# Laying the RWKV-7 units out by pairs of heads, with an issue order that counts changes of tile shape

## The chip, the core and the metric

The kernel runs on one core of a Trainium2 chip. Five engines work side by side: TensorE (PE, with its weight loads as PEld), VectorE (DVE), ScalarE (ACT), GpSimd (POOL) and the DMA queues that SyncE (SP) issues. Each engine takes its instructions in the order in which they were issued, and semaphores hold an instruction back until its inputs are there. The metric is the device time of one execution in microseconds; lower is better.

## The reference, cut to what matters

The kernel computes a two-layer trunk for 256 tokens of width 1024: an RWKV-7 time mixing with a dense SwiGLU, then a dilated attention with a mixture of experts. The change is in the time mixing, which has 16 heads of 64 columns:

```python
    def step(state, inp):
        r_t, w_t, k_t, v_t, a_t, b_t = inp
        sa = jnp.einsum('bhvk,bhk->bhv', state, a_t)
        state = state * w_t[:, :, None, :] + sa[..., None] * b_t[:, :, None, :] + v_t[..., None] * k_t[:, :, None, :]
        return state, jnp.einsum('bhvk,bhk->bhv', state, r_t)

    s0 = jnp.zeros((B, H, N, N), jnp.float32)
    _, y = lax.scan(step, s0, seq_in)
```

The kernel does not step through the 256 tokens. It takes them in chunks of 64: inside a chunk the recurrence becomes a triangular 64x64 matrix for each head that is inverted (E below), and between chunks a 64x64 state for each head is handed on (ST below).

## The kernel before, in words

All engine work goes through a small recorder, the class `Engine`, whose `call` emits the instruction; so nearly every row of the profile carries its line, L190, and rows are told apart by tile names. The recorder also keeps a planner's clock for each engine: `cost` estimates an instruction, `start` says when its inputs would be ready. The work around the change is written as tasks (Python generators) that yield the engine and the tiles that their next step needs. `spin` takes, again and again, the task whose next step could start first by that clock, and a task's order number decides ties. So the planner's estimates alone fix the order of the instructions on each engine.

In this stage `spin` runs eight units (`unit`, from L869), four at a time in four lanes; a new unit starts when a lane is free. A unit is one group of four heads (256 columns, `c_` = 0 to 3) and one half of the tokens (128 tokens, `t` = 0 or 1). A lane has one PSUM bank (`lps`). Around the units run the projections of r and v (`rv_task`, tiles x0h, x0l, x2h, x2l into mmb), four of the adaLN rows (`ada_lane` with `ada_pe`, tiles rawa and cs_act), the splitting of fp32 weights into a high and a low part (whi on ACT, wlo on DVE), the output projection (`wo_task`, tiles ygh and ygl) and what the next stage needs (`pre_task`, `pn_task`). `wo_task` begins only when the ada rows are done and `gate` is there.

A unit goes through these steps, all in 128 partitions, where the upper and the lower 64 partitions are the two chunks of 64 tokens:

- A, R, and the products BKn of b and k are made elementwise; `transpose` turns A and R into ART, and BKn into BKT. BKn is written on DVE as four pieces of 64x256.
- The scores: BKT times ART, eight products of 64 rows by 128 columns (K = 64, tile names ART,BKT). The four of one half of the rows go into the lane's bank and are masked into SM on DVE; then the four of the other half follow in the same bank.
- The inverse: E starts from SM, and four rounds of two product groups follow (T,SM into X, then E,X into E), each of eight 64x64 products, and a last round in 32x32 tiles. Chunk 0 works in array quadrant (0,0) and chunk 1 in quadrant (64,64), in turn.
- The state, chunk after chunk: SM times SV (plus ART times the state ST) gives U; E times U goes into SV; BKn times SV, added to ST and scaled by pcm, is the next ST; SM times SV plus ART times ST gives Y. The four heads of a chunk all write to the same 64 output partitions, those of the chunk.
- Y is normalized on DVE, multiplied with the gate (lga with g2t, and the last 32 rows as a product of 32 rows, tile names w2t,lw), transposed, and split into ygh and ygl.

An fp32 product of the code stands as two rows MATMUL in the trace, a transpose and a product of split weights (fp32r) as one.

Elsewhere the same recorder orders the attention stage.

## Time and profile before

| | us |
|---|---|
| three runs | 1843.07, 1843.85, 1847.41 (median 1843.85) |
| profiled execution, its own time | 1846.92 |
| its span | 1845.2 |
| PE busy | 1715.7 (93%) |
| DVE busy | 1497.0 (81%) |
| ACT busy | 1120.4 (61%) |
| POOL busy | 296.6 (16%) |

The span runs from the first to the last instruction; 1.7 us of the execution lie around it. By the tile names of the trace, the time mixing runs from about 40 us to 370 us, the dense SwiGLU to about 590, the attention to about 825, and the experts to 1835. Matmuls overlap in their pipeline and each has a row of at least 0.2 us, so a busy PE can still take more work; what a product costs in a row of equal ones is read from the distance of the starts.

### The profile page before, as it was taken

How to read it: one execution, taken by the hardware profiler on the slowest of the kernel's cores; microseconds unless marked ns; L12 is line 12 of the kernel's file. 1: busy time of each engine (PE TensorE's matmuls, PEld its weight loads, DVE VectorE, ACT ScalarE, POOL GpSimd, SP SyncE). 2: the span in 40 equal slices, each digit the busy share in tenths (PEclk: the TensorE clock that was granted, in tenths of full speed). 3: DMA queues.
4: the chain of work that ended last, by engine and by line, in shares of the span. 5: the costliest groups of instructions: out<-in, count | busy, mean ns of one | idle time of the engine just before them, and what ended most of it. 6: DMA issues, size and time to landing. Idle time of an engine off the chain costs nothing. (4 is left out here: it accounts for less than half of the span.)

```text
span 1845.2 us, 26366 instructions
## 1 busy us (share of the span) xinstructions
PE 1715.7 (93%) x9828; PEld 1368.3 (74%) x9828; DVE 1497.0 (81%) x2044; ACT 1120.4 (61%) x1447; POOL 296.6 (16%) x222
## 2 busy tenths in 40 slices
PE   6998998869998888979999999999999999999896
PEld 3676776558876666778888888888788787788674
DVE  2786786389886768579899898998888988988888
ACT  3443342236553656438777777877777777777674
POOL 0012222044532785250000000000000000000200
PEclk8998998889998999979999999999999999999998
DMA  9551153559894574568999999999999999999880
GB/s 330 155 160 30 54 164 116 150 189 357 296 354 151 194 256 154 195 230 293 334 352 368 357 349 380 348 360 332 345 368 340 352 345 349 352 344 359 311 320 24
DMA packets 213564, 498.94 MB, mean 270 GB/s; under 512 B 14634, under 2 KB 28818, under 8 KB 213428
## 3 DMA queue, kind: packets, MB, share of 16 engines
q1 hardware_dynamic: 212564, 494.03, 75.7%
q0 software_dynamic: 864, 3.15, 0.5%
q8 instruction: 79, 1.29, 0.3%
q14 instruction: 57, 0.47, 0.1%
HBM read 496.07 MB, written 1.06 MB: 269 GB/s over the span
## 5 line engine op out<-in xcount | busy, mean ns | idle before, releaser
L190 DVE TENSOR_TENSOR wlo<-raw,whi 128x1024 fp32r<-128x1024 f32 x800 | 991.6, 1277 | 138.0 <-ACT whi L190 123.7
L190 ACT CAST whi<-raw 128x1024 fp32r<-128x1024 f32 x808 | 823.9, 1048 | 291.9 <-PE mmb L190 221.2
L190 PE MATMUL mmb<-wlo,xeh 128*128 128x512 f32 x896 | 355.9, 397 | 5.9 <-DVE wlo L190 5.2
L190 PE MATMUL mmb<-whi,xeh 128*128 128x512 f32 x896 | 352.5, 394 | 0.0
L190 PE MATMUL mmb<-whi,xel 128*128 128x512 f32 x896 | 351.6, 392 | 0.0
L190 PEld LDWEIGHTS mmb<-wlo,xeh 128*128 128x128 f32 x896 | 168.4, 188 | 48.3 <-DVE wlo L190 14.9
L190 PEld LDWEIGHTS mmb<-whi,xeh 128*128 128x128 f32 x896 | 168.4, 188 | 34.2 <-ACT whi L190 0.2
L190 PEld LDWEIGHTS mmb<-whi,xel 128*128 128x128 f32 x896 | 168.4, 188 | 32.6
L190 PE MATMUL psb<-wlo,ah 128*128 128x512 f32 x448 | 176.7, 394 | 1.5 <-DVE wlo L190 1.5
L190 PE MATMUL psb<-whi,al 128*128 128x512 f32 x448 | 174.7, 390 | 0.0
L190 PE MATMUL psb<-whi,ah 128*128 128x512 f32 x448 | 161.8, 391 | 0.0
L190 POOL TENSOR_TENSOR macc<-macc,gate 128x1024 f32<-128x1024 f32 x2 | 5.7, 2889 | 924.8 <-ACT gate L190 924.8
L190 POOL TENSOR_TENSOR acc<-acc,raw 128x512 f32<-128x512 f32 (+1 forms) x62 | 128.2, 2082 | 74.2 <-DVE acc L190 42.9
L190 PEld LDWEIGHTS psb<-wlo,ah 128*128 128x128 f32 x448 | 84.1, 188 | 24.6 <-DVE wlo L190 6.2
L190 PEld LDWEIGHTS psb<-whi,ah 128*128 128x128 f32 x448 | 83.5, 188 | 18.8 <-ACT whi L190 1.6
L190 PEld LDWEIGHTS psb<-whi,al 128*128 128x128 f32 x448 | 84.2, 188 | 16.4
L190 PE MATMUL mmb<-whi,f_xl 128*128 128x512 f32 (+1 forms) x192 | 72.1, 375 | 1.1 <-DVE f_xl L190 1.1
L190 PE MATMUL mmb<-whi,f_xh 128*128 128x512 f32 (+1 forms) x192 | 72.7, 379 | 0.0
L190 PE MATMUL mmb<-wlo,f_xh 128*128 128x512 f32 (+1 forms) x192 | 72.0, 375 | 0.2 <-DVE wlo L190 0.2
L190 ACT CAST ah<-psb 128x512 fp32r<-128x512 f32 x56 | 32.6, 583 | 60.3 <-PE psb L190 60.2
L190 ACT ACTIVATE e_s<-mmb 128x512 f32<-128x512 f32 x56 | 33.5, 599 | 44.8 <-PE mmb L190 44.8
L190 DVE TENSOR_TENSOR e_s<-e_s,mmb 128x512 f32<-128x512 f32 x56 | 38.2, 683 | 22.5 <-PE mmb L190 22.2
(417 smaller groups left out, 2589.3 us busy)
## 6 DMA issues: line engine op xcount, KB each, us to landing
raw<-in_moe_w_gu_dram SPq DMA_DIRECT2D x192, 1024.0 KB, 6.6
raw<-in_moe_w_down_dram SPq DMA_DIRECT2D x83, 1024.0 KB, 6.1
raw<-in_moe_w_gu_dram SPq DMA_DIRECT2D x60, 512.0 KB, 7.0
raw<-in_moe_w_down_dram SPq DMA_DIRECT2D x56, 512.0 KB, 6.0
raw<-in_ada_w_dram SPq DMA_DIRECT2D x37, 512.0 KB, 5.3
rawa<-in_ada_w_dram SPq DMA_DIRECT2D x35, 512.0 KB, 4.2
raw<-in_ada_w_dram SPq DMA_DIRECT2D x15, 1024.0 KB, 7.8
raw<-in_ffn_w_gu_dram SPq DMA_DIRECT2D x21, 512.0 KB, 5.3
```

What stands on the lines that cost most here:

```text
L190: return fn(*a, **kw)
```

## The change

Each lane's unit keeps its tiles and its steps. What is different:

- The two halves of the partitions hold two pairs of heads in place of the two chunks. In the inverse and the state, heads 0 and 1 of a unit work in one half of the array and heads 2 and 3 in the other, so that products that follow each other alternate between the two halves. The state's BKn times SV is four products of 64 output partitions in place of two of 128, and the sums with ST and the decay are done in halves of 64x128 by DVE; pcm is gone, and GpSimd clears SV and ST.
- The products b and k are made in 128x256 (Bf, Kf) and transposed together with A and R. The scores of the two row halves go into two PSUM banks in turn (the lane's own and mmb 2, which one unit at a time may hold, `bank2`).
- BKn is now copied from Bf and Kf in eight pieces of 64x128, SV from v in four, Y from the bank in four, and the E times U result by DVE and ACT, half each.
- The gate's last 32 rows stand in a zeroed 128-row tile (xh), so that their product has the full shape.
- The ada rows are issued in pairs, 16 rows of MATMUL in one go, with order number 3.5 (103 before); the r and v projections also have 3.5.
- `wo_task` also waits until all units have their scores, and `pre_task` takes its turn for the bank mmb 2.
- The planner adds 170 ns to a product whose tile shape differs from the last one (`CHG`), adds 170 ns to the ready time of a PE step whose hinted shape differs from the current one (`SHP`), makes DVE slower while GpSimd is at work (`GPF`), and no longer discounts alternating tiles in its count of PE activity.

```diff
+    CHG, GPF, SHP = 170, 0.6, 170
...
+                shp = tuple(32 if v <= 32 else 64 if v <= 64 else 128 for v in (k, m))
+                if shp != ham.get("shape"):
+                    ham["shape"] = shp
+                    start0, start = start, start + CHG
+                    grp["all"] = max([grp["all"]] + list(grp.values())) + CHG
+                    return self.pe(op, o, passes, n, k, m, col, cold, n0, start) + CHG
...
+            for q in range(0, 8, 2):
+                rws = [ada_raw(i, q + j) for j in range(2)]
+                yield PE, "128x32", rws[0], rws[1]
...
+        yield V, ta, kkr
+        Bf, Kf = kkr, Q
+        V.scalar_tensor_tensor(Bf, ta, 1.0, kkr, op0=OP.add, op1=OP.mult)
+        yield V, k2, Q
+        V.tensor_tensor(Kf, k2, Q, op=OP.mult)
+        yield lambda: not bank2[0]
+        bank2[0] = 1
+        yield PE, "128x128", A, R, Bf, Kf
...
+        pss = [lps((128, 2, 2, 128)), mmt(2, (128, 2, 2, 128))]
+        for ch in range(2):
+            for pr in range(2):
+                for par in range(2):
+                    sl = slice(par * 64, par * 64 + 64)
+                    PE.matmul(pss[par][:, ch, pr], BKT[sl, pr, ch].rearrange("q a t -> q (a t)"),
+                              ART[sl, pr, ch].rearrange("q a t -> q (a t)"), start=True, stop=True)
...
+        def each():
+            for ch in range(2):
+                for hh in range(2):
+                    for hp in range(2):
+                        yield slice(hp * 64, hp * 64 + 64), ch, 2 * hp + hh, ch * 2 + hh
...
+                for src, d in ((Bf, hp), (Kf, 1 - hp)):
+                    e = pick([SC, V], src)
+                    yield e, src
+                    (SC.copy if e is SC else V.tensor_copy)(BKn[d * 64:d * 64 + 64, ch, cs_], src[s_, cs_])
...
+        def products(ps, ch, a, st):
+            for hh in range(2):
+                for hp in range(2):
+                    h = 2 * hp + hh
+                    PE.matmul(ps[hp * 64:hp * 64 + 64, hh], SM[:, ch, h, a * 64:a * 64 + 64],
+                              SV[:, ch, h * 64:(h + 1) * 64], start=hh == 0, stop=st is None and hh == 1)
...
+                for pr in range(2):
+                    for par in range(2):
+                        hsl = slice(pr * 128 + par * 64, pr * 128 + par * 64 + 64)
+                        PE.matmul(ps2[par * 64:par * 64 + 64, pr], BKn[:, ch, hsl], SV[:, ch, hsl], start=True,
+                                  stop=True)
...
-        PE.matmul(gps, lgb[:, tsl], w2t[96:128, csl], start=False, stop=True, tile_position=(96, 0))
+        PE.matmul(gps, lgb[0][:, tsl], w2t[:, csl], start=False, stop=True)
...
-        yield lambda: len(vsb) == 8 and "gate" in pre and not ada_left[0]
+        yield lambda: len(vsb) == 8 and "gate" in pre and not ada_left[0] and sm_n[0] == 8
...
+                if need[0] is PE and SHP:
+                    hint = next((h_ for h_ in need if isinstance(h_, str)), "128x128")
+                    at += SHP * (hint != "%dx%d" % ham.get("shape", (128, 128)))
...
-                 (103, ada_lane(LANE)), (104, pre_task()), (105, pn_task(0)), (106, pn_task(1)),
+                 (3.5, ada_lane(LANE)), (104, pre_task()), (105, pn_task(0)), (106, pn_task(1)),
```

Three places show how the order on PE moves. In the names, the number behind a tile's name is the unit (SM_0 is unit 0's SM), the last number counts tiles, psb is a lane's bank and mmb one of the four others. First PE at the scores of unit 0, before:

```order
L190 MATMUL psb_879<-a2t_266,la_268 128x256
L190 MATMUL psb_895<-ART_0_797,BKT_0_858 128x128 x4
L190 MATMUL psb_908<-sg_2_901,cst2_112 128x256
L190 MATMUL psb_914<-w2t_265,lw_267 128x256
L190 MATMUL psb_914<-a2t_266,la_268 128x256
L190 MATMUL psb_924<-ART_0_797,BKT_0_858 128x128 x4
```

And after, where the eight stand together (the last four go on as the first four):

```order
L204 MATMUL psb_960<-cst2_112,P_2_848 64x2 x4
L204 MATMUL psb_967<-ART_0_901,BKT_0_902 128x128
L204 MATMUL mmb_968<-ART_0_901,BKT_0_902 128x128
L204 MATMUL psb_967<-ART_0_901,BKT_0_902 128x128
L204 MATMUL mmb_968<-ART_0_901,BKT_0_902 128x128
```

Two runs of four into one bank each have become one run of eight that changes the bank with each product.

Second PE at the first chunk of unit 0's state, with units 1 and 2 in their inverse, before:

```order
L190 MATMUL psb_1507<-SV_0_1496,SM_0_884 64x64 x4
L190 MATMUL psb_1513<-ART_2_1195,BKT_2_1283 128x128 x4
L190 MATMUL psb_1521<-U_0_1501,E_0_956 64x64 x4
L190 MATMUL psb_1530<-T_1_1518,SM_1_1112 64x64 x8
L190 MATMUL psb_1543<-SV_0_1496,BKn_0_803 128x128 x2
L190 MATMUL psb_1550<-E_1_1322,X_1_1548 64x64 x8
L190 MATMUL psb_1561<-SV_0_1496,SM_0_884 64x64 x4
```

And after:

```order
L204 MATMUL psb_1700<-SV_0_1656,SM_0_949 64x64 x4
L204 MATMUL psb_1708<-T_1_1698,SM_1_1148 32x32 x8
L204 MATMUL psb_1721<-U_0_1662,E_0_1035 64x64 x4
L204 MATMUL psb_1726<-T_2_1717,SM_2_1390 64x64 x8
L204 MATMUL psb_1739<-E_1_1285,X_1_1707 32x32 x8
L204 MATMUL psb_1750<-SV_0_1656,BKn_0_1034 64x64 x4
L204 MATMUL psb_1765<-E_2_1456,X_2_1737 64x64 x8
L204 MATMUL psb_1782<-SV_0_1656,SM_0_949 64x64 x4
```

BKn is four products of 64 output rows in place of two of 128; the three units stand closer to each other.

Third PE at the end of the stage, unit 7's last chunk, before (ygh and ygl are the output projection, row is the end of an ada row; 90 more products of the projection follow):

```order
L190 MATMUL mmb<-rawa,cs_act 32x256 x4
L190 MATMUL psb<-U_3762,E_3443 64x64 x4
L190 MATMUL psb<-SV_3757,SM_3387 64x64 x4
L190 MATMUL psb<-ST_3809,ART_3323 64x128 x2
L190 MATMUL mmb<-rawa,cs_act 32x256 x12
L190 MATMUL mmb<-cst,row 128x128 x2
L190 MATMUL mmb<-whi,ygh 128x512
L190 MATMUL mmb<-wlo,ygh 128x512
L190 MATMUL mmb<-whi,ygl 128x512
L190 MATMUL psb<-g2t,lga 128x256
```

And after:

```order
L204 MATMUL mmb<-whi,ygl 128x512
L204 MATMUL psb<-SV_4047,BKn_3619 64x64 x4
L204 MATMUL psb<-SV_4047,SM_3507 64x64 x4
L204 MATMUL psb<-ST_3848,ART_3477 64x128 x2
L204 MATMUL psb<-SV_4047,SM_3507 64x64 x4
L204 MATMUL psb<-ST_4059,ART_3477 64x128 x2
L204 MATMUL psb<-U_4057,E_3620 64x64 x4
L204 MATMUL psb<-SV_4047,SM_3507 64x64 x4
L204 MATMUL psb<-ST_4059,ART_3477 64x128 x2
L204 MATMUL psb<-g2t,lga 128x256
L204 MATMUL psb<-w2t,xh 128x256
L204 MATMUL psb<-cst,Y_4058 128x128 x2
```

All ada rows, and 84 of the 96 products of the output projection, now stand ahead of unit 7's last transposes (cst,Y); 12 follow them.

## Rows read from the trace of the kernel before

**Rows 1.** The page, part 2: the granted TensorE clock in 40 slices.

```profile
PEclk8998998889998999979999999999999999999998
```

**Rows 2.** Windows: stretch, length, busy us of PE, PEld, DVE, ACT, POOL, PEclk.

```profile
95.00:142.00 47.00, 45.07 (x530) 38.74 (x532) 41.63 (x115) 21.35 (x53) 6.18 (x10) 1.00 0.54 163
142.00:204.00 62.00, 54.43 (x674) 43.79 (x673) 38.73 (x138) 20.00 (x55) 13.14 (x23) 0.81 0.05 13
...
296.00:346.00 50.00, 42.52 (x439) 28.66 (x438) 18.34 (x66) 11.46 (x30) 6.95 (x12) 0.77 0.47 138
70.00:370.00 300.00, 267.95 (x2951) 207.16 (x2949) 203.05 (x596) 108.84 (x260) 54.52 (x90) 0.92 0.38 115
...
95.00:370.00 275.00, 246.99 (x2821) 193.01 (x2821) 186.13 (x560) 99.02 (x241) 50.10 (x84) 0.91 0.37 112
```

**Rows 3.** Waits, 95 to 346 us: who for whom, total us, times, longest.

```profile
DVE E L190 <- PE psb L190: 21.4, 16, 4.5
...
PE mmb L190 <- DMA rawa<-in_ada_w_dram: 4.8, 3, 2.2
```

**Rows 4.** Timeline of PE, 121 us: start, length, rows*columns of the array, output.

```profile
121.10 0.68 PE L190 MATMUL psb<-T,SM 64*64 64x64 f32 x16
121.71 1.16 PE L190 MATMUL psb<-ART,BKT 64*128 64x128 f32 x8
122.80 0.68 PE L190 MATMUL psb<-E,X 64*64 64x64 f32 x16
```

**Rows 5.** Timeline of PE, 145 to 150 us.

```profile
145.36 0.71 PE L190 MATMUL psb<-SV,BKn 128*128 128x128 f32 x4
146.00 0.68 PE L190 MATMUL psb<-E,X 64*64 64x64 f32 x16
...
148.58 0.67 PE L190 MATMUL psb<-SV,SM 128*64 128x64 f32 x8
149.09 0.60 PE L190 MATMUL psb<-ST,ART 128*64 128x128 f32 x4
149.62 0.68 PE L190 MATMUL psb<-T,SM 64*64 64x64 f32 x16
```

**Rows 6.** Windows with tile kqT alone (attention): PE busy and count.

```profile
700.00:702.00 2.00, 2.00 (x38) 2.00 (x37) 0.00 (x0) 1.00 0.44 94
```

**Rows 7.** Timeline of PE in the attention, 764 us.

```profile
764.14 0.88 PE L190 MATMUL psb<-et,vv 128*64 128x128 f32 x12
764.95 0.23 PE L190 MATMUL psb<-zero 1*128 1x128 bf16 x1
```

**Rows 8.** Tiles SV, ART and U: counts, ns min/median/max, first and last start.

```profile
L190 PE MATMUL psb<-SV,SM x256: 222/222/370, 142.5 to 331.1; 128*64 128x64 f32 x128
...
L190 PE MATMUL psb<-SV,BKn x48: 275/275/582, 145.4 to 325.4; 128*128 128x128 f32 x48
...
L190 PE MATMUL psb<-ART,BKT x128: 272/272/374, 102.4 to 289.7; 64*128 64x128 f32 x128
...
L190 PE MATMUL psb<-ST,ART x96: 272/273/421, 149.1 to 331.5; 128*64 128x128 f32 x96
...
L190 PE MATMUL psb<-U,E x128: 218/218/366, 144.2 to 330.0; 64*64 64x64 f32 x128
```

**Rows 9.** Tiles E, ST and X: elementwise work on DVE and ACT.

```profile
L190 DVE COPY E<-psb x16: 271/284/290, 141.8 to 319.7; 32x128 f32<-32x128 f32 x16
...
L190 DVE TENSOR_TENSOR ST<-psb,ST x8: 385/421/425, 152.4 to 325.7; 128x256 f32<-128x256 f32 x8
...
L190 ACT COPY X<-psb x48: 257/372/378, 115.5 to 316.2; 128x256 f32<-128x256 f32 x32, 32x128 f32<-32x128 f32 x16
```

**Rows 10.** Timeline of PE at the stage's end, with idle time before and its releaser.

```profile
334.54 0.64 PE L190 MATMUL mmb<-rawa,cs_act 128*32 128x256 f32 x8 [2.16 <-DMA rawa<-in_ada_w_dram]
...
339.10 0.78 PE L190 MATMUL mmb<-whi,ygh 128*128 128x512 f32 x1
...
368.45 0.40 PE L190 MATMUL mmb<-whi,ygl 128*128 128x512 f32 x1
```

More of the change, by code (lines that the diff above doesn't have):

```diff
@@ L1039, in unit @@
             SC.copy(X, ps)
[L1040 removed]
+            yield PE, "64x64", X
             ps = lps((128, 4, 64))
[L1042 removed]
+            for sl, ch, h, j in each():
+                PE.matmul(ps[sl, j], X[sl, j], E[sl, j], start=True, stop=True)
             yield V, ps
@@ L1101, in unit @@
-            first = t == 0 and ch == 0
-            yield PE, SV
-            ps = lps((128, 4, 64))
-            for h in range(4):
-                PE.matmul(ps[sl, h], SM[:, ch, h, 0:64], SV[:, ch, h * 64:(h + 1) * 64], start=h == 0,
-                          stop=first and h == 3)
+            first, final = t == 0 and ch == 0, t == 1 and ch == 1
+            if not final:
+                sn = lt("ST", "t1", (128, 2, 128)) if ch == 0 else up.tile([128, 2, 128], F32, name=f"ST{c_ % 2}",
+                                                                           bufs=1)
+                yield GP,
+                GP.memset(sn.rearrange("p r n -> p (r n)"), 0.0)
@@ L1110, in unit @@
                 st = ST[c_]
-                yield PE, st
-                with_state(ps, sl, ch, 0, st)
-            yield SC, ps
-            SC.copy(U[sl], ps[sl])
-            yield PE, U
-            ps = lps((128, 4, 64))
-            for h in range(4):
-                PE.matmul(ps[sl, h], E[sl, h], U[sl, h], start=True, stop=True)
-            yield SC, ps
-            SC.copy(h4(SV[sl, ch]), ps[sl])
-            if not (t == 1 and ch == 1):
-                yield PE, SV
-                ps2 = lps((128, 2, 128))
+            yield PE, "128x64", SV
@@ new lines, in unit @@
+            ps = lps((128, 2, 64))
+            products(ps, ch, 0, st)
+            if st is not None:
+                yield PE, "128x64", st
+                with_state(ps, ch, 0, st)
+            js = slice(ch * 2, ch * 2 + 2)
+            yield SC, ps
+            SC.copy(U[:, js], ps)
+            yield PE, "64x64", U
+            ps = lps((128, 2, 64))
+            for hh in range(2):
+                for hp in range(2):
+                    sl = slice(hp * 64, hp * 64 + 64)
+                    PE.matmul(ps[sl, hh], E[sl, ch * 2 + hh], U[sl, ch * 2 + hh], start=True, stop=True)
@@ L1124, in unit @@
+            for hp in range(2):
+                sl = slice(hp * 64, hp * 64 + 64)
+                e = SC if hp else V
+                yield e, ps
+                (SC.copy if hp else V.tensor_copy)(SV[sl, ch, hp * 128:hp * 128 + 128],
+                                                   ps[sl].rearrange("p h n -> p (h n)"))
+            if not final:
+                yield PE, "128x64", SV
+                ps2 = lps((128, 2, 64))
                 for pr in range(2):
-                    prs = slice(pr * 128, (pr + 1) * 128)
@@ L1134, in unit @@
                 ST[c_] = sn
                 ST_n[c_] = t * 2 + ch + 1
-            yield PE, SV
-            ps = lps((128, 4, 64))
-            for h in range(4):
-                PE.matmul(ps[sl, h], SM[:, ch, h, 64:128], SV[:, ch, h * 64:(h + 1) * 64], start=h == 0,
-                          stop=first and h == 3)
+            yield PE, "128x64", SV
+            ps = lps((128, 2, 64))
+            products(ps, ch, 1, st)
             if not first:
-                with_state(ps, sl, ch, 1, st)
@@ L1143, in unit @@
-            yield SC, ps
-            SC.copy(Y[sl], ps[sl])
+                with_state(ps, ch, 1, st)
+            for hp in range(2):
+                yield SC, ps
+                SC.copy(Y[ch * 64:ch * 64 + 64, 2 * hp:2 * hp + 2], ps[hp * 64:hp * 64 + 64])
         yield GP, v_, bon
```

198 lines of the change are left out of this document (106 added, 92 removed).

## The prediction, made before the change was run

> **What bounds the kernel now.** I read the clock line of the page first, then windows over the time mixing, the waits there, and last PE's timeline at single steps. Two things are to be seen. From 95 to 370 us, 275 us that hold nearly all of what the change touches, PE is busy for 247.0 us; DVE for 186.1 and ACT for 99.0 [rows 2]. PE is thus the engine that the stage waits for most: even the copy that takes E's new part waits 21.4 us for PE, in 16 waits alone [rows 3]. And the clock is not full there. The page's line has four eights among the seven slices from the third to the ninth [rows 1]; the windows put that at 0.81 from 142 to 204 us, 0.77 from 296 to 346 us and 1.00 from 95 to 142 us [rows 2]. With two levels, 1.2 and 2.4 GHz, a mean of 0.91 over the 275 us [rows 2] is some 50 us at the lower one. So I sum PE's work, at full clock, and then ask what fills PE's idle time: 275 - 247 = 28 us.
>
> **Pairs of small products.** What does a product cost alone, and what does one cost beside another in the other half of the array? The trace shows both. In the attention, products of 64 rows by 128 columns from two heads alternate between the row halves and banks: 38 rows in 2.00 us, 0.053 us each [rows 6]. Products of 128 rows by 64 output columns alternate between column halves there: 12 rows in 0.81 us with their start, 0.067 each [rows 7]. In the stage itself eight such score rows, all in one row half, take 1.09 us to the next group's start, 0.136 each [rows 4], and four ST,ART rows, all in one column half, 0.53 us [rows 5]. So a pair runs in the time of one, and I price a row with 128 moving columns at 0.106 us alone and 0.053 paired, one with 64 columns at half of that: the 16 T,SM rows, which alternate already, take 0.61 us with the entry into their shape [rows 4], where 16 x 0.0265 is 0.42.
>
> What becomes paired, with counts from [rows 8]:
> - scores ART,BKT: 128 x 0.053 = 6.8 us saved;
> - SV,SM: 256 x 0.0265 = 6.8;
> - ST,ART: 96 x 0.053 = 5.1;
> - U,E: 128 x 0.0265 = 3.4;
> - SV,BKn: 48 x 0.106 = 5.1 before; 96 paired rows of 64 columns after, 2.5: 2.5 saved.
>
> Sum 24.6 us. The inverse (T,SM and E,X) alternates before and after: nothing.
>
> Here a page of the skill speaks for less. The rows above give a factor of two for two halves. The Trainium skill, TensorE: Matmul & The Clock Gate, section Measured speedup vs the span model, lists 3.07 times for four row tiles and 2.38 times for three column tiles, under four fifths of the ideal; by that my estimate for two tiles is 1.56 times, the saving 17.7 us in place of 24.6, and the forecast below some 7 us higher. The trace of this case differs [rows 6, 7], and I go by it.
>
> **Changes of tile shape.** Between the stage's first product and the last of the output projection, PE's program changes its tile shape 245 times before and 172 times after, counted in the two orders. The price of one is what groups take over their rows: 0.61 - 0.42 = 0.19 us for T,SM and 1.09 - 0.85 = 0.24 for the scores (in and out, halves of two changes each) [rows 4]; 0.64 - 0.42 = 0.22 for SV,BKn, and for the two ends of a run of 128x64 products, 0.51 - 0.42 = 0.09 going in and 0.53 - 0.42 = 0.11 going out [rows 5]. I take 0.17; the ends 0.09 and 0.24 give 6.6 and 17.5. 73 fewer x 0.17 = 12.4 us. PE's work falls by 24.6 + 12.4 = 37.0, to 210 us. That the gate's last product gets the full shape is in this count.
>
> **What the other engines get.** DVE loses 32 pieces of 64x256 for 16 of 128x256, 16 x 0.42 us saved, and the 20 state steps of 128x256 become 40 halves of 64x128; it gains ten copies of 128x256 out of the bank and 19 of 64x128. Rows of 128x256 take 0.421 us and of 32x128 0.284 [rows 9]; a 64x128 piece holds as much per partition as the second, so I take 0.284 with 0.42 as the other end: 4.2 + 5.4 + 11.4 - 8.4 - 6.7 = +5.9 us, at most +13.9. From 70 to 370 us DVE is busy 203 of 300 us [rows 2]; 209 still leaves it free. ACT gets 61 copies of 64x128 for BKn, 0.26 to 0.37 us each by the small and the large X copy [rows 9], 16 to 23 us beside 108.8 of 300 [rows 2]: hidden in the sum. But the eight stand in a row on ACT ahead of a unit's SV copies and of X copies of other lanes. They don't need E and can run while its last steps do; where that cover is gone, they hold a unit for 2 us. I charge 3 us for the stage, ends 0 and 16. GpSimd's clears replace pcm's; it is busy 54.5 of 300 us [rows 2], nothing.
>
> **The ada rows in pairs.** There are two buffers. Before, one is filled while the other is used; now a pair takes both, so the next pair's loads start only when PE has used the last. PE waits for them up to 2.16 us before the change [rows 10], 4.8 us in three waits [rows 3]. Behind a waiting pair on PE stand all lanes. 16 pairs come; that some are placed early by the planner I charge with 3 us, ends 0 and 16 x 2 = 32. In return the rows are done earlier, since their order number lies ahead of the units' now.
>
> **The output projection.** Before, its 96 products start when the last ada row is through, and run from 339.1 to 368.7 us [rows 10], with unit 7 nearly done. Now 84 of them stand between steps of units 5 to 7, whose chains leave PE gaps. It is the same PE work, 29.6 / 96 = 0.31 us each with some at the lower clock [rows 10], up to 26 us for 84; it is worth at most the idle time that it fills. I count it as the reason why idle time does not grow as PE's share falls.
>
> **Sum.** 275 = 247 + 28 becomes 210 + 28 + 3 + 3 = 244, 31 us less. The attention's order changes too (61 changes of shape become 64, 14 more of the products that keep the clock up); I price it at nothing, with one tenth of a 46 us slice of the clock line, 4.6 us, as the end on either side. Everything behind the stage starts earlier by as much. Against the profiled execution: 1846.9 - 31 = 1815.9; this execution lies 3.1 us over the median, so I forecast 1843.85 - 31 = 1813 us.
>
> **Rivals.**
> - *The gaps close as well.* The projection fills 16 of the remaining 34 idle us, and the denser stretch at 296 to 346 us keeps the higher clock: 210 + 18 = 228, 47 less, 1797. For it: idle and low clock stand in that stretch together [rows 2]. Against it: the earlier low stretch, 142 to 204, gets no such filler.
> - *DVE is next.* From 95 to 142 us DVE is busy 41.6 of 47 us [rows 2], beside a full PE. If the waits between the engines hold DVE to 0.75 over the whole stage, 209 / 0.75 = 279 us in place of 300: 21 less, 1823. Against it: DVE's mean is 0.68 and its share in 142 to 204 only 0.62. The Trainium skill, TensorEngine Tiling (Array Packing), section PSUM Bottleneck, says that tiling speeds up the products and not the copies out of PSUM; this rival is that rule at work.
> - *The pairs of ada rows wait.* Each of 16 pairs waits about 2 us, as at 334.5 us [rows 10], with everything behind it: 32 us, the whole gain; 1844, no change. Against it: PE's own waits for these rows were three before, 4.8 us in all [rows 3].
> - *The change does not pair.* Where a half waits for its own input, products of the two halves don't overlap; then only the shapes count: 12.4 - 6 = 6 less, 1838. Against it: in the new order both halves read one tile, written by one step.
> - *The clock falls*, and the kernel is slower. Shorter products leave the chains' waits as they are, so in 142 to 204 and wherever only chains run, PE idles more and gets 1.2 GHz for longer. At 0.91 the low share is 0.18; the 247 busy us are then about 225 at full clock, 188 after. The stage takes 188 / (1 - s/2) + 28 for a low share s: equal to before at s = 0.48, and at s = 0.6 it takes 296 us, 21 more: 1865. It decides above one half of the stage. For it: the clock falls in just these stretches [rows 2]. Against it: a third of the stage would have to join them.
>
> **How the numbers follow.** Forecast 0.40; gaps close 0.20; DVE next 0.20; does not pair 0.05; ada pairs wait 0.07; clock falls 0.08. About 0.3% (5.5 us) is what a measurement of this kernel can tell from no change. At 1838 the fourth is just past that bound and counts as faster. Faster: 0.40 + 0.20 + 0.20 + 0.05 = 0.85. Same 0.07, slower 0.08. The range leaves out the last two and a little at the lower end: from 1787, where idle falls to 8 us (210 + 8 = 218, 57 less), to 1838.
>
> **What would show it.** Right: ART,BKT rows 16 in about 1 us and SV,SM rows 8 in 0.3; PE busy in the stage down by some 37 us; the output projection's last 12 products about 5 us behind unit 7's end; the experts starting some 30 us earlier. Wrong: those rows paired but PE's idle time up by as much (chains or DVE), long waits of cs_act for DMA rawa, or a mean clock in the stage under 0.8.

## The result, and the profile after

The changed kernel takes 1837.33 us, the median of 8 runs (1829.65 to 1840.53), against 1847.35 for the kernel before in 8 runs beside them. The ratio is 0.9944, with a 95% interval of 0.9927 to 0.9962: 10 us faster, a third of the 31 us that were forecast. The profiled execution of the changed kernel took 1840.5 us, its span is 1838.7. It is the longest of its eight, and what is split up below is one execution of each kernel, so lengths and clock losses can lie some us off the medians.

The granted clock in 40 slices, to be read beside [rows 1], has three eights and a seven among the seven slices from the third to the ninth, in place of four eights:

```profile
PEclk8999988789998998989999999999999999999998
```

Windows of the changed kernel, with the columns of [rows 2] (busy us of PE, PEld, DVE, ACT, POOL, then PEclk):

```profile
95.00:142.00 47.00, 42.20 (x493) 38.27 (x493) 39.92 (x107) 20.11 (x47) 7.23 (x9) 0.96 0.50 157
142.00:204.00 62.00, 53.56 (x904) 45.56 (x899) 44.90 (x142) 32.25 (x101) 10.14 (x19) 0.94 0.29 100
296.00:346.00 50.00, 38.67 (x405) 28.32 (x403) 27.51 (x81) 20.52 (x59) 5.42 (x10) 0.82 0.25 74
70.00:370.00 300.00, 241.71 (x3017) 188.62 (x3016) 220.63 (x651) 124.94 (x352) 57.34 (x75) 0.88 0.39 123
95.00:370.00 275.00, 219.63 (x2875) 174.74 (x2874) 205.13 (x613) 115.05 (x330) 53.73 (x71) 0.87 0.36 115
```

PE's busy time from 95 to 370 us fell from 247.0 to 219.6 us, but the clock fell with it, from 0.91 to 0.87, and the stage did not become shorter by as much. Before the stage's end the largest change is from 204 to 247 us. Before and after:

```profile
204.00:247.00 43.00, 40.47 (x448) 33.99 (x446) 33.79 (x93) 18.56 (x44) 12.91 (x21) 1.00 0.46 145
```

```profile
204.00:247.00 43.00, 33.20 (x427) 24.67 (x427) 37.65 (x132) 15.50 (x50) 10.13 (x14) 0.84 0.50 157
```

PE idles 9.8 of these 43 us after and 2.5 before, and the granted clock is 0.84 where it was 1.00. Waits from 95 to 346 us, as in [rows 3]:

```profile
PE psb L204 <- DVE T L204: 5.3, 7, 2.3
DVE E L204 <- PE psb L204: 5.2, 9, 1.1
PE psb L204 <- ACT X L204: 4.7, 7, 1.5
PE psb L204 <- DVE ST L204: 4.1, 4, 1.3
PE psb L204 <- ACT SV L204: 3.8, 5, 1.4
PE psb L204 <- DVE Sc L204: 3.5, 5, 0.9
PE psb L204 <- ACT Y L204: 3.4, 6, 1.0
PE mmb L204 <- DMA rawa<-in_ada_w_dram: 1.6, 2, 1.0
```

E waited 21.4 us for PE before, 5.2 now; and PE waits longer for the steps that write T, X, ST, SV, Sc and Y between its products, each of them on DVE or ACT. For the first four of them the kernel before has, from 70 to 400 us:

```profile
PE psb L190 <- DVE T L190: 2.7, 3, 1.7
PE psb L190 <- DVE ST L190: 2.2, 3, 1.0
PE psb L190 <- ACT X L190: 1.0, 1, 1.0
PE psb L190 <- ACT SV L190: 0.5, 1, 0.5
```

That is 6.4 us together, and 17.9 after. The ada rows, which now come in pairs, wait less than before, 1.6 us against 4.8.

To compare whole stages I take a mark behind them: from 70 us to the 49th product of the SwiGLU stage (f_x). From there to the end of that stage the two kernels run alike, 11.3 us apart throughout. One window for each kernel ends at that mark, before at 399.2:

```profile
70.00:399.20 329.20, 284.03 (x3015) 219.73 (x3014) 228.20 (x649) 114.81 (x267) 70.81 (x97) 0.91 0.37 111
```

and after at 388.0:

```profile
70.00:388.00 318.00, 257.34 (x3069) 200.40 (x3068) 233.60 (x677) 131.14 (x362) 63.57 (x79) 0.88 0.37 117
```

PE's idle time is the length less the busy time: 45.2 us before, 60.7 after. Of the busy time, 50.6 us before and 61.3 after lie in stretches granted 1.2 GHz (worked out from all PE rows and the stretches of the granted clock; a 128x512 product starts every 0.23 us at the higher level and every 0.42 at the lower, in the tail shown below, so I count half of such time as lost). That splits the stage in three:

| | length | PE's work at full clock | lost to the lower clock | PE idle |
|---|---|---|---|---|
| before | 329 | 259 | 25 | 45 |
| after | 318 | 227 | 31 | 61 |
| difference | -11 | -32 | +5 | +16 |

So 32 of the 37 us of work that were forecast to go did go, and two thirds of them came back as idle time and as lower clock. Sorted by the product that ends it, the idle time ahead of the products of the units' chains (the inverse and the state) grew from 11.0 to 29.3 us, all other idle time went from 34.2 to 31.4. Behind the stage the attention takes 2.8 us more than before (from the last product of the SwiGLU stage to the first product P,hn 236.9 against 234.1), so that the experts start 8.5 us earlier; and from there to the end it takes 2.0 us more. So the two profiled executions are 6.4 us apart, the medians 10.0.

### The profile page after: what moved, and what is told of

It reads as the page before. It is cut to its first block, busy times and chain, and to the rows that moved or that the text cites. A ratio compares the mean times of both kernels' runs of the same rounds, so it can differ in the third digit from the quotient of the medians.

```text
span 1838.7 us, 26568 instructions
## 1 busy us (share of the span) xinstructions
PE 1695.5 (92%) x9890; PEld 1352.9 (74%) x9890; DVE 1500.2 (82%) x2077; ACT 1134.6 (62%) x1536; POOL 293.7 (16%) x206
## 5 line engine op out<-in xcount | busy, mean ns | idle before, releaser
L204 DVE TENSOR_TENSOR wlo<-raw,whi 128x1024 fp32r<-128x1024 f32 (+1 forms) x799 | 993.0, 1281 | 142.5 <-ACT whi L204 128.4
```

Source lines behind the costliest of these rows:

```text
L204: return fn(*a, **kw)
```

## Experiments

Times are medians beside runs of the kernel before on the same chip; the work, clock loss and idle time of each profiled execution, from 70 us to the same mark, stand in one table. They are made as in the table above, and can differ by a unit from the length by rounding. The last four columns are of one execution each: the profiled one of filled_gaps is 10 us shorter than its median, those of old_orders_pool, before_two_products, before_x_twice and no_alternation 3 to 6.

| kernel | us | ratio to before (95%) | length | work | clock loss | idle |
|---|---|---|---|---|---|---|
| before | 1847.35 | 1 | 329 | 259 | 25 | 45 |
| after | 1837.33 | 0.9927 to 0.9962 | 318 | 227 | 31 | 61 |
| wo_late | 1836.99 | 0.9912 to 0.9954 | 316 | 225 | 30 | 61 |
| old_costs | 1837.35 | 0.9907 to 0.9963 | 322 | 232 | 36 | 54 |
| old_orders | 1834.38 | 0.9903 to 0.9952 | 313 | 230 | 19 | 65 |
| before_new_costs | 1848.06 | 0.9981 to 1.0024 | 333 | 251 | 28 | 53 |
| no_low_split | 1841.75 | 0.9945 to 0.9985 | 322 | 225 | 27 | 70 |
| low_split_twice | 1845.03 | 0.9950 to 0.9990 | 327 | 226 | 35 | 66 |
| two_products | 1822.08 | 0.9803 to 0.9889 | 306 | 201 | 39 | 65 |
| filled_gaps | 1873.25 | 1.0089 to 1.0173 | 344 | 250 | 34 | 61 |
| bkn_pool | 1836.12 | 0.9924 to 0.9964 | 313 | 227 | 24 | 62 |
| bkn_twice | 1854.92 | 1.0035 to 1.0074 | 330 | 226 | 33 | 70 |
| x_twice | 1843.24 | 0.9965 to 0.9997 | 324 | 228 | 29 | 67 |
| old_orders_pool | 1832.96 | 0.9911 to 0.9953 | 309 | 228 | 20 | 61 |
| before_two_products | 1810.07 | 0.9776 to 0.9839 | 289 | 240 | 13 | 36 |
| before_x_twice | 1838.57 | 0.9946 to 0.9976 | 318 | 262 | 17 | 39 |
| all_relief | 1820.88 | 0.9830 to 0.9893 | 299 | 203 | 32 | 64 |
| no_alternation | 1840.44 | 0.9951 to 0.9998 | 320 | 233 | 23 | 64 |
| layout_only | 1848.39 | 0.9986 to 1.0015 | 331 | 229 | 36 | 66 |
| layout_only_two | 1837.50 | 0.9921 to 0.9963 | 318 | 206 | 48 | 65 |

The idle column tells most: 36 to 53 us in the four kernels with the old layout, 54 to 70 in the sixteen with the new one. The difference lies ahead of the products of the chains: 9 to 11 us of idle time with the old layout and 22 with the new costs on it; 22 to 35 with the new layout and 16 with the old costs on it. All other idle time is 27 to 34 us with the old and 30 to 40 with the new layout.

**The projection, the costs, the order numbers.**

```diff
-        yield lambda: len(vsb) == 8 and "gate" in pre and not ada_left[0] and sm_n[0] == 8
+        yield lambda: len(vsb) == 8 and "gate" in pre and not ada_left[0] and sm_n[0] == 8 and done.get((2, 3), 0) == 2
```

> The changed kernel, but the output projection may start only when the last unit is done, so that none of its 96 products stands between the steps of units 5 to 7 (84 do in the changed kernel, and unit 7 ends at 354 us there, 343 before). Three theories. (a) The projection's products hold up the inverses of units 6 and 7, which take 47 and 42 us in the changed kernel and 30 and 29 before: unit 7 ends some 12 us earlier, near 342, the 96 products then take about 25 us, the projection ends near 367, and the kernel is some 7 us slower than the changed one, 1844. (b) The products only fill PE's waits and cost the units nothing: unit 7 ends at 354 again, the projection at 379, 1857. (c) PE's work alone sets the stage: the units end 20 us or more earlier, the projection ends at 359 as now, 1837.

It came out at 1836.99, as (c) had it. The edit is weaker than the text above says: its wait ends a little before unit 7's end, so that the products start at 325.5 us and 33 of them (84 in the changed kernel) still stand ahead of unit 7's last transposes. These come at 335.6 us, 18.5 us earlier than in the changed kernel:

```profile
325.49 0.99 PE L204 MATMUL mmb<-whi,ygh 128*128 128x512 f32 x1
...
335.60 0.44 PE L204 MATMUL psb<-cst,Y 128*128 128x128 f32 x2 [0.65 <-DVE Y L204]
335.79 0.48 PE L204 MATMUL mmb<-whi,ygh 128*128 128x512 f32 x1
...
355.02 0.40 PE L204 MATMUL mmb<-whi,ygl 128*128 128x512 f32 x1
```

So the products that stand between the steps of units 5 to 7 in the changed kernel cost the units what they save at the end: the idle time is 61 us in both, and in wo_late the long wait stands behind the projection:

```profile
PE psb L204 <- DVE u L204: 10.1, 2, 9.4
```

In the changed kernel it stands ahead of the projection's end. There, beside [rows 10], PE waits 7.94 us for unit 7, and the last 12 products begin at the lower clock, 0.42 us apart, and end at the higher one, 0.23 apart:

```profile
354.09 0.69 PE L204 MATMUL psb<-cst,Y 128*128 128x128 f32 x2 [7.94 <-DVE Y L204]
355.24 0.79 PE L204 MATMUL mmb<-whi,ygh 128*128 128x512 f32 x1 [0.46 <-ACT ygh L204]
...
358.22 0.63 PE L204 MATMUL mmb<-whi,ygh 128*128 128x512 f32 x1
358.64 0.46 PE L204 MATMUL mmb<-wlo,ygh 128*128 128x512 f32 x1
...
359.41 0.39 PE L204 MATMUL mmb<-wlo,ygh 128*128 128x512 f32 x1
359.64 0.40 PE L204 MATMUL mmb<-whi,ygl 128*128 128x512 f32 x1
```

```diff
-    CHG, GPF, SHP = 170, 0.6, 170
+    CHG, GPF, SHP = 0, 0, 0
...
-                ham["n"] += passes * n * k / 128
+                ham["n"] += passes * n * k / (128 if not alt else 256 if m > 32 else 512)
```

> The changed kernel, its layout kept, but the planner's costs as before: nothing for a change of tile shape, no hint of the shape in the choice of the next step, DVE not slowed by GpSimd's clock. (a) The costs hold the units up by waiting for a like shape: without them the units end earlier although there are more changes, about 5 to 10 us faster than the changed kernel, 1828 to 1832. (b) The costs are worth their 73 fewer changes at 0.17 us: PE's work in the stage is up by about 12 us and the kernel 5 to 12 us slower, 1842 to 1849. (c) The stage is set by the units' chains of steps whatever the order: within 3 us of 1837.

```diff
-            yield 3.5, PE, hi, lo, xl, ps[0], ps[1]
+            yield PE, hi, lo, xl, ps[0], ps[1]
...
-        yield lambda: len(vsb) == 8 and "gate" in pre and not ada_left[0] and sm_n[0] == 8
+        yield lambda: len(vsb) == 8 and "gate" in pre and not ada_left[0]
...
-                 (3.5, ada_lane(LANE)), (104, pre_task()), (105, pn_task(0)), (106, pn_task(1)),
+                 (103, ada_lane(LANE)), (104, pre_task()), (105, pn_task(0)), (106, pn_task(1)),
```

> The changed kernel, but with the order numbers of before: ada rows at 103, r and v projections at 100, and the projection doesn't wait for the units' scores. (a) The rows put ahead of the units are what lengthened unit 0's inverse from 35 to 44 us and those of the others, and ate the gain: units end 10 us earlier, 1827. (b) The early ada rows are what lets the projection fill PE's waits: without them the ada rows end as late as before (about 337 us), the projection stands behind unit 7, and the kernel is 5 to 10 us slower, 1842 to 1847. (c) The numbers matter little, within 3 us of 1837.

Both stay at the changed kernel's time, answer (c). With the old costs PE changes shape 221 times between the marks in place of 170, and its work is 6 us more, about 0.11 us for a change, but it idles 7 us less. The old order numbers run with less of the lower clock (51 us of 313, against 79 of 318) and idle more.

The costs on the kernel before (the lines of the planner, and the hints at its steps):

> The kernel before, its layout kept, with the planner's new costs (170 ns for a change of tile shape, the hints of the shapes at the steps of the units and of the ada rows, DVE slowed by GpSimd's clock). (a) The costs alone bring what the change brings: about 1837. (b) The layout brings it and the costs save only part of the changes of shape: 3 to 8 us faster than before, 1840 to 1844, with PE busy in the stage only little less than the 247 us of before. (c) The costs order the attention worse, which gives back 2 to 3 us there: 1845 to 1852.

1848.06 is in the range of (c), but not by its reason: the attention takes 233.8 us there, no more than before. The changes of shape fell from 243 to 169 and the work by 8 us (0.10 us for a change, by this pair of kernels), and all of it went into idle time, 8 us more, and clock, 3 us more.

**Loads and reliefs of one engine.**

```diff
             yield V, rw, hi
-            V.tensor_tensor(lo, rw, hi.bitcast(F32), op=OP.subtract)
+            if kind == "k":
+                V.tensor_tensor(lo, rw, hi.bitcast(F32), op=OP.subtract)
+            else:
+                V.tensor_tensor(lo[:, 0, 0:16], rw[:, 0, 0:16], hi[:, 0, 0:16].bitcast(F32), op=OP.subtract)
+                lo = hi
```

> DVE relieved. The changed kernel, but for the 24 weight pieces of the r, v and output projections DVE subtracts 16 columns in place of 1024 and the products take the high part in place of the low one (so the low part of these weights is left out of the result). PE, ACT and DMA do the same work; DVE does 24 x 1.2 = 29 us less, beside the units and not in their chains. (a) DVE is the engine that holds the stage (204 to 247 us: busy 37.7 of 43): 12 to 25 us faster than the changed kernel, 1812 to 1825. (b) PE's work or its clock holds it: within 4 us, 1833 to 1841. (c) The units' chains of dependent steps hold it: within 4 us as well.

And the line that is taken away here made twice:

> DVE loaded. The changed kernel, but each of the 24 subtractions that make the low part of a weight piece (128x1024, 1.2 us) is made twice: 29 us more for DVE in the stage, none for the others. (a) DVE holds the stage: 12 to 29 us slower than the changed kernel, 1849 to 1866. (b) PE or its clock, or (c) the chains: under 8 us slower, 1837 to 1845.

DVE isn't the bound: 22 us less of it made the kernel 4 us slower, where (a) has 12 to 25 us faster, and 28 us more made it 8 us slower, short of (a) and at the end of what (b) and (c) have.

```diff
-                    mm3(ps[t], xh[:, kk, tsl], xl[:, kk, tsl], hi[:, k], lo[:, k], kk == 0 and t == 0, kk == 7 and t == 1)
+                    PE.matmul(ps[t], xh[:, kk, tsl], hi[:, k], start=kk == 0 and t == 0, stop=False)
+                    PE.matmul(ps[t], xl[:, kk, tsl], hi[:, k], start=False, stop=kk == 7 and t == 1)
```

> PE relieved. The changed kernel, but the r, v and output projections leave out the product of the high part of the input with the low part of the weight (the low part is still made): 128 rows of 256 columns and 32 of 512 less, by their starts in the trace about 128 x 0.116 + 32 x 0.23 = 22 us of PE in the stage, none for the others. (a) PE's work holds the stage: 15 to 22 us faster than the changed kernel, 1815 to 1822. (b) DVE or the chains hold it: under 6 us faster, and PE idles 15 us more. (c) The clock falls with the lighter load and eats the gain: within 3 us, with a granted clock in 95 to 354 us below the 0.87 of the changed kernel.

15 us, at the edge of (a). In the stage alone 25 us of work gave 12: idle time grew by 4 us and the clock took 8.

```diff
+    def keep_clock1(at):
+        while len(ksb) == 2 and not bank2[0] and not ops_ and clk["PE"] + GAP1 < at:
+            PE.matmul(mmt(2, (128, 256)), identr[:, 0:128], identr, start=True, stop=True)
```

> The clock fed. The changed kernel, with 125 useless 128x256 products (0.116 us each, 15 us) where the planner sees PE wait over 0.1 us for the next step, before the output projection starts. (a) The lower clock (78 us at the lower level from 70 us to the SwiGLU stage, 61 before) is what ate the gain: granted clock in 95 to 354 us above 0.92, and 5 to 12 us faster than the changed kernel, 1825 to 1832. (b) PE's own work holds the stage: 5 to 15 us slower. (c) Chains or DVE hold it and the clock hardly matters: within 3 us.

It is 36 us slower by the medians, more than any of the three theories has; the profiled execution is 22.5 us slower, its stage 26, with busy time at full clock up by 24 and idle time as it was. The trace has 91 of these products in the stage, not 125 (the other 34 rows with their tile, identr into mmb, belong to the attention, which has such products in the changed kernel too). So each of them added 24 / 91 = 0.26 us to PE's busy time, where the text above has 0.116. The planner's gaps are not the chip's. The clock theory was not tested by it, as the idle time was not filled.

**The copies that the layout adds.**

```diff
-                    e = pick([SC, V], src)
-                    yield e, src
-                    (SC.copy if e is SC else V.tensor_copy)(BKn[d * 64:d * 64 + 64, ch, cs_], src[s_, cs_])
+                    yield GP, src
+                    GP.tensor_copy(BKn[d * 64:d * 64 + 64, ch, cs_], src[s_, cs_])
```

> The changed kernel with the 64 copies of 64x128 that make BKn on GpSimd (61 of them on ACT before this edit, 16.5 us there, in rows of eight ahead of a unit's SV). (a) These copies are what PE waits for: its waits for ACT, 20 us from 70 us to the SwiGLU stage against 9 before, fall by half, and the kernel is 6 to 12 us faster than the changed one, 1825 to 1831. (b) They are hidden, and the waits come from the units' own steps: within 4 us of 1837. (c) GpSimd's work slows DVE beside it and makes BKn late: 3 to 10 us slower.

> The changed kernel with every BKn copy made twice, on the engine that the planner picks: some 64 x 0.27 = 17 us more, nearly all on ACT, nothing more for PE. (a) ACT's rows of copies stand in the way of PE: 8 to 17 us slower than the changed kernel, 1845 to 1854. (b) They are hidden beside the inverse: within 4 us, 1833 to 1841.

They are hidden, as (b) of the first has it, but the cover ends there: twice as many cost 17.6 us by the medians, just above (a) of the second and all that was added (ACT's instructions sum to 17 us more); 13 us by the profiled executions. The X copies twice (the line SC.copy(X, ps) doubled):

> The changed kernel with the 32 copies of X in the inverse (128x256, 0.37 us, ACT) made twice: 12 us more on ACT, each in the chain of a unit between two groups of products; nothing more for PE. (a) The units' chains of dependent steps set the stage, two units in a row on each of four lanes: each unit has four such copies, so 8 x 0.37 = 3 us more if the chains run side by side, up to 12 us if PE waits for each one: 1840 to 1849. (b) PE's work alone sets it and other units' products fill the wait: within 2 us, 1835 to 1839.

6 us, inside (a), but see the same edit on the kernel before, below. Old orders with both kinds of copies on GpSimd (the two edits above, and GP.tensor_copy for the SV copies from v):

> The order numbers of before (ada rows 103, r and v 100, no wait of the projection for the scores; 1834.4 alone) together with the BKn copies and the four SV copies of each unit on GpSimd, 26 us off ACT. (a) Both edits help and add up: 1822 to 1829. (b) ACT's copies are hidden, so it stays at 1834 give or take 3. (c) GpSimd is slower at them and the units wait for SV: 1838 to 1845.

1832.96 is the shortest time of a full computation here, but its interval overlaps that of the changed kernel and of old_orders: answer (b).

**The same edits on the kernel before.**

> The kernel before with the r, v and output projections leaving out the product of the high part of the input with the low part of the weight, as was done on the changed kernel: some 25 us of PE's work at full clock gone, nothing else. On the changed kernel that gave 15 us. (a) Before the change PE's work set the stage one for one, and idle time stood still as the forecast had it: 22 to 25 us faster than before, 1822 to 1825. (b) PE's idle time and its clock gave back a good part already before: 10 to 16 us faster, 1831 to 1837.

35 us, more than either theory. The window to the mark for the kernel before with two products:

```profile
70.00:358.60 288.60, 252.87 (x2860) 190.88 (x2859) 225.88 (x640) 117.90 (x275) 71.93 (x98) 0.93 0.41 128
```

The same window for the changed kernel with two products:

```profile
70.00:375.70 305.70, 240.69 (x2909) 183.96 (x2908) 231.03 (x675) 132.25 (x364) 64.50 (x79) 0.83 0.38 121
```

Work fell by 19 us, and idle time and clock loss fell too, by 9 and 12. So the omitted work alone does not account for the 35 us: the order was redrawn as well, and 72 rows of products on ada rows now stand from 142 to 204 us, where the kernel before has none. With the same omission the old layout is 12 us faster than the new one, although it has 38 us more work at full clock.

> The kernel before with the 32 copies of X in the inverse (0.37 us, ACT) made twice: 12 us more in the units' chains, nothing more for PE. On the changed kernel that cost 6 us. (a) Before, PE's longer work of other units hid the units' own waits, and only the shorter work has laid them bare: under 2 us slower, 1846 to 1849. (b) The waits stood on the path before too: 4 to 8 us slower, 1851 to 1855.

Slower was expected either way; it is 7 to 9 us faster. The edit itself can't speed anything up: it redraws the planner's order. The last ada row is at 313.5 us in place of 337.6, and the projection starts at 315.0 in place of 339.1. So a single edit's difference under some 10 us can't be put down to the edit, here and above. This holds for the change itself: a redrawn order brings the old layout to 1838.57 us, 1 us from the changed kernel. Its stage is as long, with 35 us more work, 14 us less lost to the clock and 22 us less idle time. What the change is worth against the old layout in its best order is thus not shown by the 10 us.

> The changed kernel with both reliefs at once: the r, v and output projections without the low part of the weight (25 us of PE's work; 15 us faster alone), and BKn and the SV copies on GpSimd (26 us off ACT; 1 us faster alone for BKn). (a) With PE relieved, ACT's copies are next, so that their relief is now worth more: 20 us or more faster than the changed kernel, below 1818. (b) The units' chains and the order are the rest, ACT is no bound: 13 to 18 us, 1819 to 1824.

> The changed kernel with the order of products inside a step turned: first all products of one half of the array, then those of the other (four and four for the scores, two and two for SV,SM, U,E and SV,BKn), so that only one pair in the middle overlaps. Tiles, copies and steps stay. (a) The pairs are worth their time at PE: scores 3 of 8 slots of 0.053 us x 16, the groups of four one slot of 0.027 to 0.053 us each (88 groups of SV,SM, U,E and 24 of SV,BKn), 7 us in all for the sum by the forecast; 5 to 9 us slower than the changed kernel. (b) The stage gives PE's time back at half: 2 to 5 us slower. (c) The chains set it: within 2 us.

all_relief adds nothing to two_products, answer (b). no_alternation adds 6 us to PE's work, near the 7 that were forecast for the pairs that it undoes, and 3 us to the kernel, answer (b), inside what a redrawn order does. But the 6 us are not where the forecast had them. Nearly all of them are the scores, whose rows took 9.4 us from start to start and now take 14.8:

```profile
106.34 0.82 PE L204 MATMUL psb<-ART,BKT 64*128 64x128 f32 x5
106.90 0.37 PE L204 MATMUL mmb<-ART,BKT 64*128 64x128 f32 x1
107.00 0.27 PE L204 MATMUL psb<-ART,BKT 64*128 64x128 f32 x1
...
107.33 0.72 PE L204 MATMUL mmb<-ART,BKT 64*128 64x128 f32 x5
107.98 0.40 PE L204 MATMUL psb<-cst,P 128*64 128x2 f32 x8
```

All eight rows of one half (psb) stand ahead of the eight of the other (mmb) in the program, and by their starts the last of the first still run beside the first of the second; the whole takes 1.64 us where the alternating order takes 1.09. The groups of eight SV,SM rows, which come as four and four, take 0.29 us to the next group in both kernels (means at the higher clock, 20 and 18 groups). So for these groups the gain comes from the use of both halves, and the order inside the group adds nothing.

**The layout alone.** This takes the layout of the changed kernel with everything on order from the kernel before: the edits of old_costs and old_orders, and the ada rows one by one.

> The layout part of the change alone: pairs of heads in the two halves, two banks for the scores, the gate's full shape; order numbers, the planner's costs and the single ada rows as in the kernel before. (a) The layout carries the gain and the new order adds nothing: within 3 us of the changed kernel, 1834 to 1840. (b) The layout's shorter products pay in full when the order is the old one: 1815 to 1828. (c) The layout gains nothing without the new order: 1843 to 1850.

> The layout alone as in the run beside it, and the r, v and output projections without the product with the low part of the weight (25 us of PE's work). With the same omission the kernel before came to 1810 and the changed one to 1822. (a) With PE relieved, the new layout's own steps between the engines (idle time 61 to 65 us from 70 us to the SwiGLU stage in every variant of it, 36 in the kernel before with the same omission) set the stage whatever the order: 1817 to 1825, slower than the old layout. (b) It was the new order that cost the 12 us: 1805 to 1812. (c) The layout's smaller work shows in full: below 1800.

The layout alone gains nothing, answer (c), with 30 of the 32 us of work saved. Its window to the mark:

```profile
70.00:401.10 331.10, 265.39 (x3067) 203.85 (x3067) 230.89 (x684) 129.94 (x356) 60.42 (x78) 0.85 0.36 112
```

PE is busy 18.6 us less than in the kernel before, at a lower clock, 0.85 for 0.91, and idles 66 us for 45. With two products it is 27 us behind the old layout with the same omission. That is the side of (a), and slower than it had. So the idle time comes with the layout, without the new order too (the new costs on the old layout make 8 us of it as well). The three parts of the order together make up the 11 us between this kernel and the changed one, which is hardly more than what a redrawn order does; neither the costs nor the order numbers carry them alone (old_costs, old_orders). What the order does shows from 142 to 204 us, when mostly chains run. Windows of PE's products on ada rows alone (tile rawa: length, busy us with count, granted clock), for the kernel before:

```profile
142.00:204.00 62.00, 0.00 (x0) 0.81 0.05 13
```

For the layout alone:

```profile
142.00:204.00 62.00, 0.00 (x0) 0.81 0.09 25
```

And for the changed kernel:

```profile
142.00:204.00 62.00, 3.21 (x48) 0.94 0.29 100
```

The changed kernel also has 120 rows of the r and v projections there (tiles x0h, x0l, x2h, x2l), the kernel before 18, the layout alone 37. These products wait for no step of a unit and run while the units copy; with them the clock is at 0.94. The old layout shows the same where its order puts such rows there, as with two products:

```profile
142.00:204.00 62.00, 5.66 (x72) 0.97 0.41 131
```

Over all twenty profiled executions, the four with the fewest rows of both kinds in this stretch (18 to 48) were granted 0.70 to 0.81, the ten with the most (136 to 181) 0.92 to 1.00, the six between them 0.78 to 1.00. It is not the whole story of the clock: from 296 to 346 us the changed kernel has none of these rows and 0.82, but the kernel before has 104 rows of ada there and 0.77.

## Why the prediction was wrong in size

The sign was right, but the forecast of 1813 was 24 us too low. That the time lies inside the range is luck: its upper end, 1838, is 0.7 us away, and it was set by a rival (the change does not pair) that the trace excludes. By the prediction's own steps:

- **PE bounds the stage.** Right in direction, not one for one. With two products the kernel before became 35 us faster for 19 us of work; on the changed kernel 25 us less work gave 12 us in the stage, and 24 us more cost 26.
- **Pairs, 24.6 us.** Right. The rows of the five groups, from each start to the next and without idle time, sum to 69.5 us before and 42.9 after, 26.6 us less (with the changes of shape at their ends, and at the clock that they had): scores 17.3 to 9.4, SV,SM 19.1 to 12.2, ST,ART 13.7 to 9.7, U,E 10.6 to 6.1, SV,BKn 8.8 to 5.5. The timeline of PE shows it, beside [rows 4, 5]:

```profile
161.97 0.27 PE L204 MATMUL psb<-ART,BKT 64*128 64x128 f32 x1
161.98 0.27 PE L204 MATMUL mmb<-ART,BKT 64*128 64x128 f32 x1
162.09 0.27 PE L204 MATMUL psb<-ART,BKT 64*128 64x128 f32 x1
162.09 0.27 PE L204 MATMUL mmb<-ART,BKT 64*128 64x128 f32 x1
...
173.22 0.45 PE L204 MATMUL psb<-SV,SM 128*64 128x64 f32 x8 [0.68 <-DVE Sc L204]
173.47 0.42 PE L204 MATMUL psb<-ST,ART 128*64 128x128 f32 x4
173.69 0.43 PE L204 MATMUL psb<-SV,SM 128*64 128x64 f32 x8
```

  Two score rows start within 0.01 us, the next two 0.11 us later; SV,SM x8 takes 0.25 us to the next group where it took 0.51. By these rows two halves give a factor of about two. The lower factor that was worked out from the Trainium skill, TensorE: Matmul & The Clock Gate, section Measured speedup vs the span model, does not agree with them.
- **Changes of shape, 12.4 us.** Counted rightly, 243 to 170 between the marks, and too dear: old_costs and before_new_costs put a change at 0.11 and 0.10 us, not 0.17, so the 73 are worth 8 us, which with the 24.6 for the pairs fits the 32 by which the work fell.
- **DVE +5.9, ACT +16 to 23, ada pairs +3.** Measured +5 (253 to 258 us, single instructions added up), +20 (124 to 144), and 3 us less waiting. DVE next is ruled out by no_low_split; long waits for pairs did not come.
- **Idle time.** This is the step that failed: the projection as "the reason why idle time does not grow as PE's share falls". The sum carried 28 us of idle time over unchanged, with 6 us for copies and pairs, and nothing for the clock. Idle time grew by 16 us, and the clock took 5 more. 84 products of the projection do stand ahead of unit 7's end and the last 12 end 5 us behind it as forecast, but wo_late shows that this is worth nothing: the units end as much later. The idle time was looked for at the stage's end, and it arises all through it, ahead of the products of the chains (11 to 29 us). That PE idles more and gets the lower clock for longer is what the rival "the clock falls" says, with a low share of 0.25 of the stage (79 of 318 us; 0.19 before), far from the 0.48 at which it would have turned the sign. It named 142 to 204 us first, and there the clock rose, from 0.81 to 0.94, where the new order has put products that wait for no unit. With the layout alone the low share is 0.30, and 21 us of idle time and 11 of clock eat the 30 us of saved work.
- **Order at 3 + 3 us and otherwise nothing.** The layout without any of the new order gives 0, and so do the planner's costs without the layout; but old_costs and old_orders each keep the whole gain, so no single part of the order is shown to carry it.
- **Attention priced at nothing, 4.6 us on either side.** 2.8 us slower, inside; in the other variants this stage takes 231.7 to 239.2 us, so its order is redrawn too. The 2.0 us behind it had no term: the experts take 1028.8 to 1030.5 us in the sixteen kernels with the new layout, 1027.1 to 1027.9 in the four with the old one.

**What stays open.** Why the chains leave more idle time is not shown. The likely reason is argued: a unit alternates between products and copies, and with shorter products less work of other units covers the copies. The rows split it in two. Ahead of the state's products PE idles 2 to 5 us with the old layout (10 with the new costs on it) and 11 to 20 with the new one; this part goes with the layout, but the state's copies also became more and smaller, and no run has the one without the other. Ahead of the inverse's products, which are the same in both layouts, it idles 3 to 8 us with the old layout (12 with the new costs) and 10 to 17 with the new one, but 4 with the old costs on it; this part moves with the order too. BKn's copies alone are not the cause (bkn_pool), nor is DVE's sum (no_low_split). The pairs of ada rows, which old_costs and old_orders both keep, were not tried alone. With orders redrawn by each edit, differences of a few us between the variants are not explained here.

## What to carry to other kernels

Don't count work taken from the busiest engine one for one: here 32 us less gave 11 in the stage. Before adding up savings, ask what runs in the stretches that hold only dependent chains, and try to keep work that depends on nothing (here ada rows, r and v) for just these. Filling the end of a stage with such work gains nothing if it delays the chain that ends last (wo_late). Where a planner draws the order anew with each edit, run a null edit or two first, to see how far the time moves by the order alone.

## What the runs showed of the hardware

Two score products in opposite row halves of the array, in two PSUM banks, start within 0.01 us of each other, and a pair of rows takes 0.11 us, as long as one row of one half alone (in no_alternation, from start to start). When all products of one half stand ahead of those of the other (no_alternation), only the last and first of them overlap for the scores, 1.64 us in place of 1.09; two and two products into the column halves lose nothing, 0.29 us in both orders. A change of tile shape cost 0.10 to 0.11 us (two pairs of kernels that differ in the order). A useless 128x256 product put where the planner saw a gap added 0.26 us to PE's busy time (filled_gaps), where such products in a row start every 0.12 us.
